# Seven products for eight in one chunk of each feed-forward product, with column blocks in pairs over eight PSUM banks, in a decoder block on Trainium2

## The chip, the cores and the metric

The kernel runs on one core of a Trainium2 chip. The metric is the device time of one execution in microseconds (us), the median of several runs. Engines are called by the names of the profile: PE (TensorE matmuls), PEld (its weight loads), DVE (VectorE), ACT (ScalarE), POOL (GpSimd), SP (SyncE, which issues most DMAs).

## The reference

One decoder block on 256 tokens of width 2048, in float32. It has two mixers side by side, a sigmoid-gated merge, an output projection, a residual and a SwiGLU feed-forward of hidden width 5632, then a final norm. The change sits in the feed-forward:

```
x1 = x + hybrid_mixer(rmsnorm(x, attn_norm_w), ...)           # 256 x 2048
h  = rmsnorm(x1, ffn_norm_w)
x2 = x1 + (silu(h @ w_gate) * (h @ w_up)) @ w_down            # 2048 -> 5632 -> 2048
out = rmsnorm(x2, final_norm_w)
```

## The kernel before

All large products run as one stream on PE. An operand `a` of a float32 product is kept as a high part (rounded to `fp32r`) and a low part (the rest), and `three` (L131) adds three products, high by high, high by low and low by high, into one PSUM bank. `Product` describes 512 output columns: for both token tiles (128 tokens each) it sums over row blocks of 128 rows of the weight, so one row block is 2 x 3 matmuls of 128 x 128 by 128 x 512. `ORDER` lists the products of the mixers; four products `wo0` to `wo3` follow, and then the feed-forward in three parts of 4, 4 and 3 hidden blocks of 512. In each part, for every hidden block `f_`, the gate product `fg` and the up product `fu` run one after the other over 16 row blocks. Four down products `fd` then run over the row blocks of that part only, and are added to the residual tiles `x1`.

`Feed` supplies the weights: `load` (L229 to L240) brings four row blocks of 512 columns (1 MB) by one DMA from SP into `wr`, of which there are three buffers. `split` (L242 to L262) takes two row blocks at a time: ACT casts them to the high part `wh` (L254) and DVE subtracts to get the low part `wl` (L255); of each there are five buffers. `split_to` keeps the splits four ahead of the products (`AHEAD`).

All else is cut into steps by generators. `Side.tick` is called after each row block, so after every six matmuls, and lets each waiting task take a step; `yield n` skips n ticks. What the traced program lists is the order on every engine: each engine runs its instructions exactly in that order, and semaphores do the rest.

A result with tokens on partitions (`g`, `x1`, `y`, the heads) has to be transposed before it can be the next product's operand. `across_task` (L158) does it in one of two ways. `transpose_task` sends eight 128 x 128 transposes through PE. `turn_task` (L182), for the kinds in `TURN`, uses `turn` (L171): 16 DVE transposes of 32 partitions x 256 elements that put each 32 x 32 block where it belongs, and then a cast on ACT and a subtraction on DVE (L189, L190; with a column scale L195, L196). `Split.ready` says when an operand is there, and `Side.until` holds back the issue of matmuls until it is.

PSUM is split into three pools: four banks for accumulators (`accp`), two for transposes (`trp`), two for attention (`atp`). `fg_done` and `fu_done` (L882 to L896) read the accumulators straight from PSUM: ACT applies silu into `g`, and DVE multiplies by the up product (L894). `fd_done` adds into `x1` (L912).

## Time and profile before

| what | value |
|---|---|
| median of 3 runs | 1752.54 us |
| lowest and highest run | 1752.49 and 1752.93 us |
| span of the profiled execution | 1750.4 us (its own time is not listed apart; the three runs lie 2.1 to 2.5 us above this span) |
| PE busy | 1739.8 us, 99% of the span, 7873 matmuls |
| DVE busy | 1217.4 us, 70% |
| ACT busy | 856.6 us, 49% |
| POOL busy | 6.3 us |
| DMA | 332.08 MB, mean 190 GB/s |
| granted PE clock | 0.9 or more of full speed in all 40 slices |

The span is the time from the first to the last instruction. Busy shares are averages over the stages. PE's matmuls are pipelined: one is listed with a length of 389 ns, but the next starts earlier, so the rate is read from starts and not from lengths.

### The profile page before, as it was taken

What the parts mean: (1) busy time and instruction counts of PE and PEld (TensorE: products, weight loads), DVE (VectorE), ACT (ScalarE), POOL (GpSimd) and SP (SyncE); (2) the same over time, 40 slices, a digit from 0 to 9 for tenths busy, and PEclk for the clock granted to TensorE, in tenths of its full rate; (3) what the DMA queues carried; (4) which work ended last, traced back from release to release, by engine and by line L of the source; (5) the groups of instructions that cost most, each with busy time, mean ns of one, the idle gap of its engine ahead of it and who ended that gap; (6) DMA issues with size and microseconds to landing.
All of it is one profiled execution on the core that took longest, in us unless ns stands there. A gap on an engine that the chain in (4) does not pass through costs nothing.

```text
span 1750.4 us, 20353 instructions
## 1 busy us (share of the span) xinstructions
PE 1739.8 (99%) x7873; PEld 1443.0 (82%) x7873; DVE 1217.4 (70%) x1838; ACT 856.6 (49%) x1103; POOL 6.3 (0%) x31
## 2 busy tenths in 40 slices
PE   9999999999999999999999999999999999999998
PEld 7888888888888888888888888888888888888886
DVE  6876877875567978876597886666546666546655
ACT  7555565644345555565444554444344444344443
POOL 1000000000000000000000000000000000000000
PEclk9999999999999999999999999999999999999999
DMA  8656555655666556555666566665566665566553
GB/s 265 215 174 192 163 174 172 180 192 195 193 194 179 175 167 187 169 172 181 212 217 204 192 206 203 193 192 193 193 194 192 194 196 195 194 193 195 196 185 106
DMA packets 169872, 332.08 MB, mean 190 GB/s; under 512 B 7584, under 2 KB 9264, under 8 KB 169776
## 3 DMA queue, kind: packets, MB, share of 16 engines
q1 hardware_dynamic: 169744, 330.78, 59.8%
q8 instruction: 61, 1.00, 0.2%
q14 instruction: 35, 0.29, 0.0%
q10 hardware_dynamic: 32, 0.01, 0.0%
HBM read 328.67 MB, written 2.10 MB: 189 GB/s over the span
## 4 chain that ended last, share of the span: by engine, by line
PE 99%; DMA 0%; DVE 0%; SPq 0%; ACT 0%; issue 0%; DVEq 0%
PE acc_fd L135 5%; PE acc_fg L134 5%; PE acc_fg L133 5%; PE acc_fu L134 5%; PE acc_fu L133 5%; PE acc_fd L133 5%; PE acc_fu L135 5%; PE acc_fg L135 5%; PE acc_fd L134 5%; PE acc_mv L133 2%; PE acc_mo L133 2%; PE acc_dq L133 2%; PE acc_gm L133 2%; PE acc_gd L133 2%; PE acc_dq L135 2%; PE acc_dk L135 2%
## 5 line engine op out<-in xcount | busy, mean ns | idle before, releaser
L255 DVE TENSOR_TENSOR wl_fg<-wr_fg,wh_fg 128x1024 fp32r<-128x1024 f32 x88 | 107.8, 1225 | 85.3 <-ACT wh_fg L254 84.7
L255 DVE TENSOR_TENSOR wl_fu<-wr_fu,wh_fu 128x1024 fp32r<-128x1024 f32 x88 | 107.6, 1225 | 80.8 <-ACT wh_fu L254 80.3
L254 ACT CAST wh_fg<-wr_fg 128x1024 fp32r<-128x1024 f32 x88 | 93.0, 1057 | 142.1 <-PE acc_fu L135 66.5
L255 DVE TENSOR_TENSOR wl_fd<-wr_fd,wh_fd 128x1024 fp32r<-128x1024 f32 x82 | 100.1, 1225 | 89.7 <-ACT wh_fd L254 89.6
L254 ACT CAST wh_fd<-wr_fd 128x1024 fp32r<-128x1024 f32 x82 | 86.2, 1056 | 122.1 <-PE acc_fd L135 96.1
L254 ACT CAST wh_fu<-wr_fu 128x1024 fp32r<-128x1024 f32 x88 | 92.6, 1054 | 96.4 <-PE acc_fg L135 48.5
L133 PE MATMUL acc_fg<-wh_fg,x1Th 128*128 128x512 f32 x352 | 136.9, 389 | 0.0
L134 PE MATMUL acc_fg<-wl_fg,x1Th 128*128 128x512 f32 x352 | 136.9, 389 | 0.0
L135 PE MATMUL acc_fg<-wh_fg,x1Tl 128*128 128x512 f32 x352 | 136.9, 389 | 0.0
L133 PE MATMUL acc_fu<-wh_fu,x1Th 128*128 128x512 f32 x352 | 136.9, 389 | 0.0
L134 PE MATMUL acc_fu<-wl_fu,x1Th 128*128 128x512 f32 x352 | 136.9, 389 | 0.0
L135 PE MATMUL acc_fu<-wh_fu,x1Tl 128*128 128x512 f32 x352 | 136.9, 389 | 0.0
L133 PEld LDWEIGHTS acc_fg<-wh_fg,x1Th 128*128 128x128 f32 x352 | 66.1, 188 | 13.7
L135 PEld LDWEIGHTS acc_fg<-wh_fg,x1Tl 128*128 128x128 f32 x352 | 66.1, 188 | 13.7
L133 PEld LDWEIGHTS acc_fu<-wh_fu,x1Th 128*128 128x128 f32 x352 | 66.1, 188 | 13.7
L135 PEld LDWEIGHTS acc_fu<-wh_fu,x1Tl 128*128 128x128 f32 x352 | 66.1, 188 | 13.7
L134 PEld LDWEIGHTS acc_fu<-wl_fu,x1Th 128*128 128x128 f32 x352 | 66.1, 188 | 13.7
L134 PEld LDWEIGHTS acc_fg<-wl_fg,x1Th 128*128 128x128 f32 x352 | 66.1, 188 | 13.6
L178 DVE STREAM_TRANSPOSE turned<-g 32x256 f32<-32x256 f32 x160 | 69.7, 435 | 2.5
L255 DVE TENSOR_TENSOR wl_bm<-wr_bm,wh_bm 128x1024 fp32r<-128x1024 f32 x32 | 39.2, 1225 | 37.4 <-ACT wh_bm L254 37.3
L178 DVE STREAM_TRANSPOSE turned<-tok_dqk 32x256 f32<-32x256 f32 x128 | 55.7, 435 | 2.1
L254 ACT CAST wh_bm<-wr_bm 128x1024 fp32r<-128x1024 f32 x32 | 33.8, 1056 | 46.6 <-PE acc_bm L135 42.4
(378 smaller groups left out, 4611.4 us busy)
## 6 DMA issues: line engine op xcount, KB each, us to landing
wr_fg<-in_w_ffn_gate_dram SPq DMA_DIRECT2D x44, 1024.0 KB, 5.2
wr_fu<-in_w_ffn_up_dram SPq DMA_DIRECT2D x44, 1024.0 KB, 5.2
wr_fd<-in_w_ffn_down_dram SPq DMA_DIRECT2D x44, 1024.0 KB, 5.1
wr_mo<-in_w_in_dram SPq DMA_DIRECT2D x16, 1024.0 KB, 5.5
wr_mv<-in_w_in_dram SPq DMA_DIRECT2D x16, 1024.0 KB, 5.4
wr_gm<-in_w_in_dram SPq DMA_DIRECT2D x16, 1024.0 KB, 5.4
wr_bm<-in_w_branch_m_dram SPq DMA_DIRECT2D x16, 1024.0 KB, 5.1
wr_dq<-in_w_in_dram SPq DMA_DIRECT2D x16, 1024.0 KB, 5.4
```

The source lines that it names most:

```text
L133: nc.tensor.matmul(o, lhsT=a[0], rhs=b[0], start=first, stop=False)
L134: nc.tensor.matmul(o, lhsT=a[0], rhs=b[1], start=False, stop=False)
L135: nc.tensor.matmul(o, lhsT=a[1], rhs=b[0], start=False, stop=last)
L178: nc.vector.transpose(out=o, in_=i)
L254: nc.scalar.copy(out=hi[:, i:i + step], in_=r)
L255: nc.vector.tensor_tensor(out=lo[:, i:i + step], in0=r, in1=hi[:, i:i + step].bitcast(F32), op=ALU.subtract)
```

## The change

Four things are done to the feed-forward, and one to all transposed results.

1. Products in pairs. `Pair` takes two column blocks at a time: gate and up of the same hidden block (11 pairs `fgu0` to `fgu10`), and two down blocks (`fd00`, `fd02`, `fd10`, `fd12`, `fd20`). The last two down blocks of the last part stay single products.
2. Seven for eight. In one chunk of four row blocks (the first), the operand's 2 x 2 quarters (two token tiles by two halves of the chunk) times the weight's 2 x 2 quarters (two halves by two column blocks) are computed as seven products of quarters or of sums of quarters (`SEVEN`), each in its own bank, P1 to P7; the other chunks add their plain products into P1 and P7 (first column block) and P2 and P8 (second). The order interleaves one of the seven with one plain operation until the seven are used up. Sums of weights are made in place in `wr` by DVE (`sum_up`, four per pair), sums of the operand by `add_up` (four additions, one cast, one subtraction, for chunk 0 of `x1T` and of each part's `gT`).
3. Evictions. `quarters` copies P3 on ACT, makes four combinations of P3 to P6 on DVE and four more DVE operations with P1, P7, P2 and P8, before silu and the multiplication (or the addition into `x1`).
4. Banks and buffers. At `fgu0` the three PSUM pools are closed and one pool of eight banks (`bankp`) is opened. `wr` has four buffers in place of three, the pool `c4` 23 in place of 25. The last hidden block's result, which went through PE transposes (`glast3`), is now of a kind in `TURN`. The final norm's weights are loaded before `fd20` and not before the first gate product.
5. `turn_task`. In place of 16 transposes of 32 partitions there are two of 128 partitions x 512 elements, which leave each 32 x 32 block on its old partitions. POOL then writes the tile to a DRAM buffer with one DMA and reads it back with four, which puts the blocks on their new partitions. The task waits four ticks between writing and reading and four between reading and use. This is done for 30 results; the two convolution inputs keep the 16 transposes.

```diff
-N_C4 = 25
+N_C4 = 23
+N_RAW = 4
+TURN_OUT, TURN_BACK = 4, 4
...
+    def feed_forward_banks():
+        banks.close()
+        late.append(ctx.enter_context(tc.tile_pool(name="bankp", bufs=8, space=PS)))
...
+        def add_up(self, g, block):
+            z = c4([P, 4, 2, P], "sums")
...
+            a11, a12, a21, a22 = (block(t, h) for t in range(2) for h in range(2))
+            for o, x, y, op in ((out[0], a12, a22, ALU.add), (out[1], a21, a22, ALU.subtract),
+                                (out[2], out[0], a21, ALU.subtract), (out[3], a11, out[2], ALU.subtract)):
+                nc.vector.tensor_tensor(out=o, in0=x, in1=y, op=op)
...
+            nc.scalar.copy(out=self.shi[g], in_=z)
+            nc.vector.tensor_tensor(out=self.slo[g], in0=z, in1=self.shi[g].bitcast(F32), op=ALU.subtract)
...
     def turn_task(src, dst, g, scale_col=None, rate=2):
-        yield 1
-        t = c4([P, 4, S], "turned")
-        yield from turn(src, t, rate)
+        yield 1
+        y = c4([P, 4, 4, TT, 32], "turned")
+        for tt in range(TT):
+            nc.vector.transpose(out=y[:, :, :, tt].rearrange("p b k s -> p k b s"),
+                                in_=src[:, tt].rearrange("p (k b f) -> p k b f", k=4, f=32))
+            yield
+        d = drp.tile([4, 32, 4, 256], F32, tag="d", name="across")
+        nc.gpsimd.dma_start(out=d.rearrange("a f b n -> (a f) (b n)"), in_=y.rearrange("p b k t s -> p (b k t s)"))
+        del y
+        yield TURN_OUT
+        t = c4([P, 4, 4 * TT, 32], "across")
+        for b in range(4):
+            nc.gpsimd.dma_start(out=t[32 * b:32 * b + 32].rearrange("p a u s -> p a (u s)"),
+                                in_=d[:, :, b].rearrange("a f n -> f a n"))
+        yield TURN_BACK
         hi, lo = dst.alloc(g)
...
+    SEVEN = (("P3", (0, 1), None, (0, 1)), ("P1", (0, 0), None, (0, 0)), ("P2", (1, 0), None, "d"),
+             ("P4", (1, 0), (1, 1), "a"), ("P5", (1, 1), (0, 1), "b"), ("P6", (0, 1), (1, 0), "c"),
+             ("P7", (0, 0), (0, 1), (1, 0)))
...
+        def sum_up(self):
+            if self.add and not self.added:
+                o, x = (feed.raw[g][:, 2 * h:2 * h + 2] for g, h in ((self.raw, self.half), self.add))
+                nc.vector.tensor_tensor(out=o, in0=o, in1=x, op=ALU.add)
+            self.added = True
+
+        def split(self):
+            self.sum_up()
...
+            nc.scalar.copy(out=hi, in_=r)
+            nxt = feed.units[feed.nsplit + 1:feed.nsplit + 2]
+            if nxt and isinstance(nxt[0], Op):
+                nxt[0].sum_up()
+            nc.vector.tensor_tensor(out=lo, in0=r, in1=hi.bitcast(F32), op=ALU.subtract)
...
+        def run(self):
+            side.push("post", self.post(self))
+            u0 = feed.units.index(self.ops[0])
+            for n, op in enumerate(self.ops):
+                feed.split_to(u0 + n + self.ahead)
+                g = op.chunk - self.g0
+                side.until(lambda: self.xt.ready[g], self.name)
+                hi, lo = op.parts
+                for j in range(2):
+                    for b, x in op.uses:
...
+                        three(self.banks[b], self.xt.quarter(g, x, j), (hi[:, j], lo[:, j]), first, self.left[b] == 0)
...
+                    if len(op.uses) == 2 or j == 1:
+                        side.tick()
...
+    def quarters(pair):
...
+        nc.scalar.copy(out=s3, in_=ps["P3"])
+        yield from pair.after("P6", 2)
+        op(u, s3, ps["P6"], ALU.subtract)
+        op(v, u, ps["P4"], ALU.add)
+        yield
+        op(x, v, ps["P5"], ALU.subtract)
+        op(u, ps["P5"], u, ALU.subtract)
+        for t, c, b, o, op_ in ((0, 0, "P1", s3, ALU.add), (1, 0, "P7", v, ALU.subtract),
+                                (0, 1, "P2", u, ALU.add), (1, 1, "P8", x, ALU.add)):
+            yield from pair.after(b, 2)
+            op(o, ps[b], o, op_)
+            yield t, c, o
```

The order of the instructions is moved everywhere in the feed-forward. Three places follow; the line numbers are each kernel's own, and the words in brackets are the engines (or DMA queues, DMASW for POOL's) that a row waits for.

First, PE where the feed-forward begins. `acc_wo3_1` is the accumulator of the last product ahead of it, `x1T` the operand. Before:

```order
L135 MATMUL acc_wo3_1_8341<-wh_wo3_8403,yTl3_7879 128x512
L133 MATMUL acc_fg0_0_8515<-wh_fg0_8427,x1Th0_8117 128x512 [waits Activation_49]
L134 MATMUL acc_fg0_0_8515<-wl_fg0_8428,x1Th0_8117 128x512 [waits DVE_49]
L135 MATMUL acc_fg0_0_8515<-wh_fg0_8427,x1Tl0_8118 128x512
L133 MATMUL acc_fg0_1_8516<-wh_fg0_8427,x1Th0_8117 128x512
```

Of the change:

```order
L181 MATMUL acc_wo3_1_8228<-wh_wo3_8294,yTl3_7807 128x512
L179 MATMUL acc_fgu0_P3_8400<-wh_fgu0_8317,x1Th0_8045 128x512 [waits DVE_49,Activation_49]
L180 MATMUL acc_fgu0_P3_8400<-wl_fgu0_8318,x1Th0_8045 128x512
L181 MATMUL acc_fgu0_P3_8400<-wh_fgu0_8317,x1Tl0_8046 128x512
L179 MATMUL acc_fgu0_P3_8400<-wh_fgu0_8317,x1Th0_8045 128x512
L180 MATMUL acc_fgu0_P3_8400<-wl_fgu0_8318,x1Th0_8045 128x512
```

The first matmul of the feed-forward now waits for DVE as well, and the one behind it, which needs DVE's `wl`, no longer has to.

Second, DVE from the end of one gate and up pair into the next (`wl` are low parts of weights, L305 sums of weights in place, `q1` and `q3` combinations, `g` the hidden block). Before:

```order
L894 SCALAR_TENSOR_TENSOR g_9013<-acc_fu1_0_9016,rs_x1_8655,g_9013 128x512 [waits PE_49]
L894 SCALAR_TENSOR_TENSOR g_9013<-acc_fu1_1_9017,rs_x1_8655,g_9013 128x512 [waits PE_49]
L255 TENSOR_TENSOR wl_fg2_9159<-wr_fg2_9072,wh_fg2_9158 128x1024 [waits DMAHW0_49,Activation_49]
L255 TENSOR_TENSOR wl_fg2_9175<-wr_fg2_9072,wh_fg2_9174 128x1024 [waits Activation_49]
L178 STREAM_TRANSPOSE turned_9186<-g_9013 32x2x4x32 [waits DVE_49]
L178 STREAM_TRANSPOSE turned_9186<-g_9013 32x2x4x32 x3
L255 TENSOR_TENSOR wl_fg2_9198<-wr_fg2_9106,wh_fg2_9197 128x1024 [waits DMAHW1_49,Activation_49]
L178 STREAM_TRANSPOSE turned_9186<-g_9013 32x2x4x32 x4
```

Of the change:

```order
L392 TENSOR_TENSOR q1_8429<-acc_fgu0_P2_8478,q1_8429 128x512
L1101 SCALAR_TENSOR_TENSOR g_8407<-q1_8429,rs_x1_8546,g_8407 128x512 [waits DVE_49]
L392 TENSOR_TENSOR q3_8431<-acc_fgu0_P8_8497,q3_8431 128x512 [waits PE_49]
L1101 SCALAR_TENSOR_TENSOR g_8407<-q3_8431,rs_x1_8546,g_8407 128x512 [waits DVE_49]
L305 TENSOR_TENSOR wr_fgu1_8677<-wr_fgu1_8677 128x1024
L317 TENSOR_TENSOR wl_fgu1_8777<-wr_fgu1_8747,wh_fgu1_8776 128x1024 [waits DMAHW7_49,Activation_49]
L317 TENSOR_TENSOR wl_fgu1_8802<-wr_fgu1_8677,wh_fgu1_8801 128x1024 [waits Activation_49]
L237 STREAM_TRANSPOSE turned_8811<-g_8407 128x4x4x32
L305 TENSOR_TENSOR wr_fgu1_8677<-wr_fgu1_8677,wr_fgu1_8605 128x1024
L317 TENSOR_TENSOR wl_fgu1_8814<-wr_fgu1_8747,wh_fgu1_8813 128x1024 [waits Activation_49]
L237 STREAM_TRANSPOSE turned_8811<-g_8407 128x4x4x32
L317 TENSOR_TENSOR wl_fgu1_8836<-wr_fgu1_8677,wh_fgu1_8835 128x1024 [waits Activation_49]
```

The evictions have doubled, sums of weights stand between the splits, and two transposes stand where there were sixteen.

Third, ACT in the first down product of the last part, where the last hidden block's operand `gT2h2` is made (`wh` are high parts of weights). Before:

```order
L254 CAST wh_fd20_13014<-wr_fd20_12928 128x1024 [waits DMAHW0_49,DVE_49,PE_49]
L254 CAST wh_fd20_13030<-wr_fd20_12928 128x1024 [waits DVE_49,PE_49]
L146 CAST gT2h2_13048<-ps_tr_13050 128x512 [waits PE_49]
L254 CAST wh_fd21_13057<-wr_fd21_12962 128x1024 [waits DMAHW1_49,DVE_49]
L254 CAST wh_fd21_13073<-wr_fd21_12962 128x1024 [waits DVE_49,PE_49]
```

Of the change, where `wh_fd20_13344` is the weight that PE multiplies with the first use of `gT2h2`:

```order
L313 CAST wh_fd20_13344<-wr_fd20_13316 128x1024 [waits DMAHW2_49,PE_49,Activation_49]
L313 CAST wh_fd20_13362<-wr_fd20_13105 128x1024 [waits DVE_49,PE_49,Activation_49]
L313 CAST wh_fd20_13375<-wr_fd20_13316 128x1024 [waits PE_49,Activation_49]
L313 CAST wh_fd20_13399<-wr_fd20_13105 128x1024 [waits DVE_49,PE_49,Activation_49]
L313 CAST wh_fd20_13412<-wr_fd20_13366 128x1024 [waits DMAHW3_49,PE_49,Activation_49]
L260 CAST gT2h2_13416<-across_13388 128x512 [waits DMASW4_49,DMASW5_49,DMASW3_49,DMASW2_49]
L260 CAST gT2h2_13416<-across_13388 128x512
```

The operand's cast waits for POOL's four DMAs instead of PE's transposes, and stands four weight casts behind the weights of its first use.

## Rows read from the trace of the kernel before

**Rows 1.** The page: busy time of each engine, and the chain that ended last by engine.
```profile
PE 1739.8 (99%) x7873; PEld 1443.0 (82%) x7873; DVE 1217.4 (70%) x1838; ACT 856.6 (49%) x1103; POOL 6.3 (0%) x31
...
PE 99%; DMA 0%; DVE 0%; SPq 0%; ACT 0%; issue 0%; DVEq 0%
```
**Rows 2.** The waits of PE: who waited <- for whom: us, times, longest.
```profile
PE ps_warm L393 <- DVE ssx L387: 1.1, 1, 1.1
```
**Rows 3.** Stages: the feed-forward: length, busy us (instructions) per engine, clock, DMA share, GB/s.
```profile
1022.40:1742.00 719.60, 719.26 (x3177) 595.39 (x3176) 445.88 (x542) 309.81 (x330) 0.00 (x0) 1.00 0.59 190
```
**Rows 4.** Timeline of PE in a down product: start us, length us, what; twelve matmuls apart.
```profile
1239.83 0.39 PE L135 MATMUL acc_fd<-wh_fd,gT0l 128*128 128x512 f32 x1
...
1242.55 0.39 PE L135 MATMUL acc_fd<-wh_fd,gT0l 128*128 128x512 f32 x1
```
**Rows 5.** Groups by form, DVE then ACT, 1064 to 1742 us: busy us, mean ns | idle before.
```profile
L255 DVE TENSOR_TENSOR wl_fu<-wr_fu,wh_fu 128x1024 fp32r<-128x1024 f32 x80 | 98.0, 1225 | 76.9 <-ACT wh_fu L254 76.4
L178 DVE STREAM_TRANSPOSE turned<-g 32x256 f32<-32x256 f32 x160 | 69.7, 435 | 2.5
L894 DVE SCALAR_TENSOR_TENSOR g<-acc_fu,rs_x,g 128x512 f32<-128x512 f32 x22 | 15.4, 744 | 0.0
L190 DVE TENSOR_TENSOR gT1l<-turned,gT1h 128x512 fp32r<-128x512 f32 x8 | 5.2, 686 | 0.0
...
L254 ACT CAST wh_fu<-wr_fu 128x1024 fp32r<-128x1024 f32 x80 | 84.3, 1054 | 92.2 <-PE acc_fg L135 48.0 <-PE acc_fu L135 44.2
L886 ACT ACTIVATE g<-acc_fg,rs_x 128x512 f32<-128x512 f32 x20 | 13.7, 690 | 9.4 <-PE acc_fg L135 9.4
L189 ACT CAST gT0h<-turned 128x512 fp32r<-128x512 f32 x8 | 4.6, 623 | 8.2 <-DVE turned L178 8.2
```
**Rows 6.** Timeline of DVE at the end of a gate and up product.
```profile
1064.54 1.23 DVE L255 TENSOR_TENSOR wl_fg<-wr_fg,wh_fg 128x1024 fp32r<-128x1024 f32 x1 [1.50 <-ACT wh_fg L254]
1065.68 1.40 DVE L894 SCALAR_TENSOR_TENSOR g<-acc_fu,rs_x,g 128x512 f32<-128x512 f32 x2
...
1069.98 1.23 DVE L255 TENSOR_TENSOR wl_fg<-wr_fg,wh_fg 128x1024 fp32r<-128x1024 f32 x1 [1.49 <-ACT wh_fg L254]
1071.12 1.78 DVE L178 STREAM_TRANSPOSE turned<-g 32x256 f32<-32x256 f32 x4
```
**Rows 7.** Timelines of ACT and of DVE: one split in a down product.
```profile
1240.25 1.06 ACT L254 CAST wh_fd<-wr_fd 128x1024 fp32r<-128x1024 f32 x1 [1.66 <-PE acc_fd L135]
...
1241.34 1.23 DVE L255 TENSOR_TENSOR wl_fd<-wr_fd,wh_fd 128x1024 fp32r<-128x1024 f32 x1 [0.30 <-ACT wh_fd L254]
```
**Rows 8.** Timeline of PE: four transposes between matmuls, in the last part.
```profile
1680.46 0.39 PE L135 MATMUL acc_fd<-wh_fd,gT2l 128*128 128x512 f32 x1
1680.70 0.60 PE L143 MATMUL ps_tr<-ident,g 128*128 128x128 f32 x4
...
1681.37 0.40 PE L134 MATMUL acc_fd<-wl_fd,gT2h 128*128 128x512 f32 x1
```
**Rows 9.** Timeline of DVE: the evictions of the last product ahead of the feed-forward.
```profile
1022.22 1.28 DVE L864 TENSOR_TENSOR x<-acc_wo,x 128x512 f32<-128x512 f32 x2
```
**Rows 10.** DMA issues: count, KB each, median us from issue to landing.
```profile
wr_fd<-in_w_ffn_down_dram SPq DMA_DIRECT2D x44, 1024.0 KB, 5.1
...
out_dram<-x SPq DMA_DIRECT2D x8, 256.0 KB, 3.1
...
fw<-in_final_norm_w_dram SPq DMA_DIRECT2D x2, 512.0 KB, 6.3
wg_raw<-in_w_in_dram SPq DMA_DIRECT2D x1, 128.0 KB, 6.2
```
**Rows 11.** DMA queue of SP (packets, MB, share of 16 engines), and what SP waited for longest.
```profile
q1 hardware_dynamic: 169744, 330.78, 59.8%
...
SPq L237 <- DVE wl_fg L255: 212.0, 42, 5.6
```
**Rows 12.** Timeline of DVE in the tail: an operation with one tensor input.
```profile
1744.15 0.88 DVE L958 TENSOR_SCALAR x<-x,f 128x512 f32<-128x512 f32 x2
```

More of the change, by code (lines that the diff above doesn't have):

```diff
@@ L1 @@
 import math
+from contextlib import ExitStack
 import concourse.bass as bass
@@ L139, in transpose_half @@
         hi, lo = dst.hi[g], dst.lo[g]
-        ps = trp.tile([P, 2, S], F32, tag="tr", name="ps_tr")
+        if late:
+            ps = late[0].tile([P, 2, S], F32, tag="bank", name="ps_tr")
+        else:
+            ps = trp.tile([P, 2, S], F32, tag="tr", name="ps_tr")
         for j in range(2):
@@ L198, in turn_task @@
+                nc.scalar.copy(out=hi[:, k:k + 2], in_=z[:, k:k + 2])
+                nc.vector.tensor_tensor(out=lo[:, k:k + 2], in0=z[:, k:k + 2], in1=hi[:, k:k + 2].bitcast(F32),
+                                        op=ALU.subtract)
             if k == 0:
                 yield
+        if g in dst.sums:
+            yield
+            if z is None:
+                dst.add_up(g, lambda tt, h: t[:, :, 4 * h:4 * h + 4].rearrange("p a (j t) s -> p t j a s", t=TT)[:, tt])
+            else:
+                dst.add_up(g, lambda tt, h: z[:, 2 * h:2 * h + 2, tt * P:(tt + 1) * P])
@@ L211, in __init__ @@
             self.hooks, self.ahead, self.by_token, self.steps = {}, AHEAD, False, {}
+    SEVEN = (("P3", (0, 1), None, (0, 1)), ("P1", (0, 0), None, (0, 0)), ("P2", (1, 0), None, "d"),
+             ("P4", (1, 0), (1, 1), "a"), ("P5", (1, 1), (0, 1), "b"), ("P6", (0, 1), (1, 0), "c"),
+             ("P7", (0, 0), (0, 1), (1, 0)))
+    class Op:
+        def __init__(self, pair, chunk, raw, half, add, uses, frees):
+            self.pair, self.chunk, self.raw, self.half, self.add = pair, chunk, raw, half, add
+            self.uses, self.frees, self.added, self.parts = uses, frees, False, None
+        def sum_up(self):
[5 more added lines that the diff above has]
+            self.sum_up()
+            r = feed.raw[self.raw][:, 2 * self.half:2 * self.half + 2]
+            hi = wp.tile([P, 2, 512], F32R, tag="wh", name=f"wh_{self.pair.name}")
+            lo = wp.tile([P, 2, 512], F32R, tag="wl", name=f"wl_{self.pair.name}")
+            nc.scalar.copy(out=hi, in_=r)
[3 more added lines that the diff above has]
+            nc.vector.tensor_tensor(out=lo, in0=r, in1=hi.bitcast(F32), op=ALU.subtract)
+            self.parts = hi, lo
+            for g in self.frees:
+                del feed.raw[g]
+                feed.load()
@@ new lines, in quarters, with op @@
+    def quarters(pair):
+        def op(o, i0, i1, op_):
+            nc.vector.tensor_tensor(out=o, in0=i0, in1=i1, op=op_)
+        ps = pair.banks
+        yield from pair.after("P3", 2)
+        s3, u, v, x = (t2([P, 512], f"q{i}") for i in range(4))
+        nc.scalar.copy(out=s3, in_=ps["P3"])
+        yield from pair.after("P6", 2)
+        op(u, s3, ps["P6"], ALU.subtract)
+        op(v, u, ps["P4"], ALU.add)
+        yield
+        op(x, v, ps["P5"], ALU.subtract)
[5 more added lines that the diff above has]
+            yield t, c, o
@@ L271, in run @@
     def run(p):
-        acc = [accp.tile([P, 512], F32, tag="acc", name=f"acc_{p.name}_{tt}") for tt in range(TT)]
+        if isinstance(p, Pair):
+            p.run()
+            return
+        acc = [bank(f"acc_{p.name}_{tt}") for tt in range(TT)]
         if p.by_token:
@@ L915, in fd_done, with down_post, task @@
         return f
+    def down_post(c, last):
+        def task(pair):
+            for got in quarters(pair):
+                if got is None:
+                    yield
+                    continue
+                t, j, q = got
+                nc.vector.tensor_tensor(out=x1[c + j][:, t], in0=x1[c + j][:, t], in1=q, op=ALU.add)
+            if last:
+                for j in range(2):
+                    side.push("fin", final_squares(c + j))
+        return task
     def weigh(c, tt):
@@ L1028, in hybrid_block @@
             side.push("param", lambda_task())
-        if p.name == "fg0":
+        if p.name == "fgu0":
+            feed_forward_banks()
+        if p.name == "fd20":
             load_fw()
```

169 lines of the change are left out of this document (124 added, 45 removed).

## The prediction

> **What bounds the kernel now.** I read the page first. PE is busy for 99% of the span, and in the chain that ended last 99% is PE and no other engine has 1% [rows 1]. Next come PE's waits: the longest is 1.1 us, at the start of the kernel, so nobody keeps PE waiting later [rows 2]. The table by stage shows that this holds in the feed-forward, where the change sits: in its 719.6 us PE is busy for 719.3, at a granted clock of 1.00, while DVE is busy for 445.9 (62%), ACT for 309.8 and the DMA engines for 59% [rows 3]. PE therefore has neither a wait nor a slow clock to give back; the feed-forward gets shorter only by fewer matmuls. Last, the groups of DVE and ACT: the idle time in front of DVE's splits ends with ACT's casts, that in front of ACT's casts with PE [rows 5], and one split shows it: ACT waits 1.66 us for PE, and DVE then 0.30 us for ACT [rows 7]. These engines follow PE and have slack. That slack must carry what the change adds.
>
> **Removed from PE.** In a down product, twelve matmuls start 1239.83 to 1242.55, so one takes 0.2267 us [rows 4]. A pair has 192 matmuls now; its first chunk of four row blocks has 48, of which seven products for eight leave 42. Sixteen pairs save 96 matmuls: 96 x 0.2267 = 21.8 us, 1.36 us per pair. A gate and up pair falls from 43.5 to 42.2 us. The eight PE transposes of the last hidden block go as well. Four of them stand between two matmuls that start 0.91 us apart in place of the 0.45 of two matmuls [rows 8]; twice 0.46 is 0.9 us.
>
> **Added at the entry.** The new pool takes over the banks of the products ahead, so PE's first matmul waits for DVE's evictions of `wo3`, which run 1.28 us from 1022.22, to 1023.5 [rows 9]. The feed-forward began at 1022.40 [rows 3]. That is +1.1 us; 0.6 if the first bank to be written is one that the first eviction freed, 2 if semaphores and a cold pipeline add to it.
>
> **Added on DVE, hidden.** Durations overlap, so I take starts: a split is followed by the next operation 1.14 us later, twice [rows 6]. Two 512-element additions from PSUM take 1.28 us [rows 9], and one lasts about 0.69 [rows 5], so they start 0.60 apart; a multiplication into `g` starts 1.40 - 0.74 = 0.66 after the one ahead [rows 5, 6]. A gate and up pair has 16 splits, 3 or 4 weight sums and three splits of summed weights, 23 operations of 1024 elements: 26.2 us. Eight combinations at 0.65 (between those two) are 5.2, two multiplications 1.3, two low parts of operands 1.2. No 128 x 512 transpose is in the trace. The four of 32 x 256 have a pitch of (1.78 - 0.435) / 3 = 0.448 us [rows 5, 6]; with twice the elements, between 0.6 (a plain 512-element operation) and eight times 0.448, that is 3.6 us. I take 0.72, near the plain operation, as such a transpose also moves one element per partition after another. The sum is 35.3 us of DVE in PE's 42.2, so I cost it at nothing; the cover is 7 us per pair, and beyond it each microsecond would cost one.
>
> The tightest place is the start of a pair. There the chain on DVE is: a cast on ACT before it (1.06 and a gap of 0.03), six operations of 1024 elements (6.8), four evictions and multiplications (2.6), two transposes (1.4): 12.0 us after the last pair's end; three more of 1024 make it 15.4, when the fifth plain split is ready. PE wants it after five of the seven products (1.36 each) and four plain operations (2.72 each): 17.7 us. The margin is 2.3 us. ACT has about 23 us of work per pair, from 19 casts at 1.06, `g` and operands [rows 5], and stays under PE. The sums of an operand (four additions, a cast and a low part) add 0.6 to 0.7 us each to DVE once per part; they come behind the fifth split, where its lead grows again, so nothing is added. The fourth buffer of `wr`, the two fewer of `c4` and the earlier load of the final weights move only work that no row shows anybody waiting for; they are costed at nothing too.
>
> **Added on POOL and the DMA queues.** Thirty results go out to DRAM (512 KB) and back, 30 MB more, so the DMA share rises from 59% to about 65%. SP waits longest for a buffer's last split on DVE (212 us over 42 times), not for bandwidth [rows 11], so the loads are not late. No DMA by POOL is in the trace. Of those by SP, 256 KB land 3.1 us after issue, 1024 KB after 5.1 [rows 10]: the way out takes 4.1. For the way back, four DMAs in short rows, I take 5.1, so the round trip is 9.2 us. Its ends: 6.2 (twice 3.1) and 12.6 (twice the 6.3 of `fw` [rows 10]); if the four came one after another, 6.3 + 4 x 6.2 = 31. It is hidden wherever the program puts the use far enough behind: writing, reading and use are eleven ticks apart, each at least six matmuls, so 15.0 us.
>
> One place has no such room: `fd20` in the last part. Its third chunk needs the hidden block that has just ended, 17.7 us after that end. The second transpose is done at 12.0, the data has landed at 21.2, the cast (0.62) and the low part (0.69) [rows 5] end at 22.5, against 18.1 (17.7 and the last matmul's own 0.39): **+4.4 us**. Even a fast trip leaves 2.6, because the operand's cast stands behind a weight cast whose buffer PE frees only at 17.7: 0.2 + 1.06 + 0.62 + 0.69. The wait is then 2.6 + (trip - 7.4); a trip of 12.6 gives 7.8. While PE waits there, ACT's and DVE's splits behind run on.
>
> On this the Trainium skill has a price: "DMA: Bandwidth & Descriptors", section "Anatomy of one DMA — SWDGE (gpsimd) path", gives a DMA by GpSimd a fixed part of some 2.0 us and the rest by bytes at 436 GB/s. As an estimate from that page each leg would take some 3 us, the wait at `fd20` would be the least one, 2.6, and the time 1733.5. No run here shows it, as POOL issues none of these before; the sum above keeps 9.2.
>
> **The sum.** -21.8 - 0.9 + 1.1 + 4.4 = -17.2 us. The profiled span of 1750.4 becomes 1733.2; runs lie 2.1 us above it, so the median of 1752.5 becomes **1735.3 us**, rounded up to 1735.5.
>
> **The rivals.**
> *A. DVE becomes the bound (slower).* Place: the two transposes in front of the next pair's splits. At 3.6 us each they add 5.8 us to the chain of 15.4, past its margin of 2.3: PE waits 3.5 us at the fifth plain split of each pair that follows a gate and up pair, 11 x 3.5 = 38 us, so 1773. It begins at 1.9 us a transpose and cancels the gain (17.2 / 11 = 1.56 us a pair) at 2.65. For it: the margin is thin, and operations that go strided through PSUM or SBUF are unseen. Against it: the transposes of 32 partitions already run near a plain operation's rate. 8%.
>
> *B. The round trip is late everywhere (slower).* ACT works in order, so an operand's cast that waits for POOL's DMAs holds back the weight casts behind it. ACT would reach it some 21.5 us after a pair's end; up to a trip of 9.5 nothing waits, up to about 15.8 the splits' lead takes it up, and beyond that each microsecond costs one in each of 11 pairs, and one at `fd20`. The gain is gone at a trip of 16.7; at 18 it is 2.2 x 11 = 24 and 8.8 at `fd20`, so 1768. For it: four DMAs in short rows, the far end of 31. Against it: all kinds of DMA rows lie between 3.1 and 6.3 us [rows 10]. 8%.
>
> The Trainium skill speaks for B in "SBUF — State Buffer", section "SBUF: two separate sides": while DVE runs an operation in its two-port mode, GpSimd cannot write the descriptors of its DMAs. This trace shows such a faster form only in the tail, where two one-input operations of 512 elements take 0.88 us [rows 12] against 0.69 for a single two-input one; between the feed-forward's transposes DVE runs two-input ones, so the rule changes little here. If it held for DVE's every operation, POOL's descriptors would come only in DVE's gaps, and the time would be that of B.
>
> *C. Part is eaten in small waits.* With seven or eight banks in use, a pair's next product finds its bank only after the combinations, and PE waits some 0.7 us (one DVE operation) at sixteen starts: +11, so 1742 to 1749. For it: the order of evictions is now longer. Against it: PE's first matmul of a later pair waits for ACT alone by the listing. 11%.
>
> *D. The saving is not there.* If the six matmuls of a quarter cost more than 0.2267 us, the 3081 that are left in the feed-forward (3177 [rows 3] less 96) take 7.1 us more for each 1.0% (0.0023 each), and 2.4% takes the whole gain: 1752. Nothing in the trace hints at it; the shapes are the same. 3%.
>
> **How the numbers follow.** My forecast has 70%. A change of 0.2% is 3.5 us, about what a measurement of this kernel can tell; so no change is 1749.0 to 1756.0. The forecast and C count as faster, and a mild A or B too: 0.70 + 0.11 + 0.02. D and half-way cases of A and B lie within 0.2%: 0.06. The rest of A and B is slower: 0.11. The range takes the short trip and the cheap entry below (1735.3 - 1.8 - 0.5, and a little less at the chunk starts: 1732.0) and the long trip (+3.4) and C above, to 1748.
>
> **What would show it.** PE has 7873 - 104 = 7769 matmuls, transposes among them, and still 0.2267 us between starts. Its waits hold one of about 1 us at the first matmul of `fgu0`, ended by DVE, and one of about 4 at `fd20`'s third chunk, ended by an operand; nothing else over 1 us. The transposes' mean is under 1.9 us; POOL's DMAs land within 4 to 5 us; DVE's busy share in the feed-forward is near 80%. I am wrong if PE waits in every pair for a low part of a weight (A) or for a high part with ACT held by POOL's DMAs (B), or if the pitch is longer (D).

## The result, and the profile after

| what | before | after |
|---|---|---|
| median of 3 runs | 1752.5 us | 1809.5 us |
| lowest to highest | 1752.5 to 1752.9 us | 1809.1 to 1814.7 us |
| profiled execution: its span | 1750.4 us | 1813.0 us |

The change makes the kernel slower: the ratio is 1.0335, with a 95% interval from 1.0316 to 1.0354. The forecast was 1735.5 us, in a range of 1732 to 1748. The profiled execution is the longest of the three, so what its trace shows adds up to some 5 us more than the medians differ by.

The page gives the busy time of each engine, and then the chain that ended last by engine:

```profile
PE 1746.1 (96%) x7769; PEld 1432.9 (79%) x7769; DVE 1262.7 (70%) x1678; ACT 911.8 (50%) x1187; POOL 88.8 (5%) x181
...
PE 75%; DVE 8%; DMA 7%; issue 7%; ACT 2%; POOL 1%; ACTq 0%; DVEq 0%; POOLq 0%
```

PE has 7769 matmuls, the number forecast, but it was 99% of the chain before [rows 1] and is 75% now. The same shows in the stage table of the feed-forward, from its start to the last matmul's start (columns as in [rows 3]):

```profile
1022.40:1803.69 781.29, 724.77 (x3073) 585.26 (x3072) 594.02 (x644) 362.02 (x405) 35.07 (x64) 0.97 0.59 192
```

The stage has grown from 719 to 781 us, with a granted clock of 0.97 where it was 1.00 [rows 3]. DVE's 594 us are 76% of it. What PE waits for (columns as in [rows 2]):

```profile
PE acc_fgu_P L180 <- DVE wl_fgu L317: 18.6, 16, 2.1
PE acc_fgu_P L179 <- ACT wh_fgu L313: 17.8, 11, 2.6
PE acc_fd_P L179 <- ACT gT2h L260: 14.5, 1, 14.5
PE acc_fd_P L180 <- DVE wl_fd L317: 2.8, 3, 1.3
PE acc_fd_P L179 <- ACT wh_fd L313: 1.8, 2, 1.4
...
PE acc_fgu_P L179 <- DVE x L1073: 1.0, 1, 1.0
```

Before, the longest wait was the 1.1 us at the start [rows 2]. Now PE waits 27 times for a low part of a weight or a high part in gate and up pairs, and once 14.5 us for the operand of the last hidden block. Behind ACT's casts stands this (the waits of ACT):

```profile
ACT wh_fgu L313 <- DVE wr_fgu L305: 96.7, 43, 4.5
...
ACT gT0h L260 <- DMA across<-across: 38.1, 4, 10.1
ACT gT1h L260 <- DMA across<-across: 36.9, 4, 9.5
ACT gT2h L260 <- DMA across<-across: 29.5, 3, 11.1
```

All 11 hidden blocks make ACT wait some 9 to 11 us for POOL's DMAs (the other, longer sum, for the weight sums on DVE, turns out below not to hold PE by itself). The first case, in the timelines of DVE, POOL, ACT and PE (start us, length us):

```profile
1082.27 0.70 DVE L237 STREAM_TRANSPOSE turned<-g 128x512 f32<-128x512 f32 x1
...
1083.27 0.56 POOL L242 DMA_DIRECT2D across<-turned  x1 [33.15 <-DVE turned L237]
1090.22 2.19 POOL L247 DMA_DIRECT2D across<-across  x4 [6.39 <-DMA across<-turned]
...
1102.04 0.62 ACT L260 CAST gT0h<-across 128x512 fp32r<-128x512 f32 x1 [9.73 <-DMA across<-across]
1102.57 1.04 ACT L313 CAST wh_fgu<-wr_fgu 128x1024 fp32r<-128x1024 f32 x1
...
1103.66 0.50 PE L179 MATMUL acc_fgu_P<-wh_fgu,x1Th 128*128 128x512 f32 x1 [1.62 <-ACT wh_fgu L313]
```

The second transpose ends at 1082.97. The way out takes until 1089.7, the four DMAs back are issued by 1091.9, and ACT gets the data at 1102.04: a round trip of 19.1 us, where 9.2 were taken. For the 11 blocks it is 17.9 to 19.2, each time up to ACT's first cast, which starts within 0.2 us of the landing. ACT then casts the weight that PE already waits for. This is rival B, at the trip that it gave as an example.

A list of the distances between PE's starts shows the whole loss. Against 0.2267 us each they are 84.9 us too long in all. 65.7 of this are single waits of over 0.25 us with the start behind them; 12.8 are 64 distances of some 0.43 us, the rate of a 1.2 GHz clock, always right after waits; here after one of 2.6 and one of 2.2 us:

```profile
1112.97 0.80 PE L180 MATMUL acc_fgu_P<-wl_fgu,x1Th 128*128 128x512 f32 x1 [2.15 <-DVE wl_fgu L317]
1113.56 0.63 PE L181 MATMUL acc_fgu_P<-wh_fgu,x1Tl 128*128 128x512 f32 x1
1113.99 0.63 PE L179 MATMUL acc_fgu_P<-wh_fgu,x1Th 128*128 128x512 f32 x1
1114.42 0.63 PE L180 MATMUL acc_fgu_P<-wl_fgu,x1Th 128*128 128x512 f32 x1
```

The granted clock of this stretch (last column but two; columns as in [rows 3]) is half of full speed:

```profile
1113.56:1117.82 4.26, 4.26 (x11) 3.34 (x10) 3.90 (x4) 0.51 (x1) 0.00 (x0) 0.50 0.86 286
```

The other 6.4 lie in distances that are only a little too long. The matmuls and transposes saved (-22.7) and these 84.9 make +62.2 of the 62.6 by which the span grew. By place: 17.0 at the last hidden block's first use, 5.2 in the first pair, about 10 in each of the three pairs that follow the first hidden block of a part, 3.1 to 4.7 in each of the seven other pairs behind a gate and up pair.

### The profile page after: what moved, and what is told of

The parts are those of the page before. It is cut to its first block, busy times and chain, and to the rows that moved or that the text cites. A ratio compares the mean times of both kernels' runs of the same rounds, so it can differ in the third digit from the quotient of the medians.

```text
span 1813.0 us, 20500 instructions
## 1 busy us (share of the span) xinstructions
PE 1746.1 (96%) x7769; PEld 1432.9 (79%) x7769; DVE 1262.7 (70%) x1678; ACT 911.8 (50%) x1187; POOL 88.8 (5%) x181
## 4 chain that ended last, share of the span: by engine, by line
PE 75%; DVE 8%; DMA 7%; issue 7%; ACT 2%; POOL 1%; ACTq 0%; DVEq 0%; POOLq 0%
DMA across<-across 5%; PE acc_fgu_P L180 3%; PE acc_fgu_P L181 3%; PE acc_fgu_P L179 3%; DVE wl_fgu L317 3%; PE acc_fd_P L180 3%; PE acc_fd_P L179 3%; PE acc_fd_P L181 3%; DMA across<-turned 2%; PE acc_mv L179 2%; PE acc_mo L179 2%; PE acc_dq L179 2%; PE acc_gm L179 2%; PE acc_dk L179 2%; PE acc_gd L179 2%
## 5 line engine op out<-in xcount | busy, mean ns | idle before, releaser
L313 ACT CAST wh_fgu<-wr_fgu 128x1024 fp32r<-128x1024 f32 x209 | 212.0, 1048 | 170.7 <-DVE wr_fgu L305 96.7
L317 DVE TENSOR_TENSOR wl_fgu<-wr_fgu,wh_fgu 128x1024 fp32r<-128x1024 f32 x209 | 250.7, 1219 | 52.9 <-ACT wh_fgu L313 49.9
L180 PE MATMUL acc_fgu_P<-wl_fgu,x1Th 128*128 128x512 f32 x594 | 237.9, 401 | 18.6 <-DVE wl_fgu L317 18.6
L179 PE MATMUL acc_fgu_P<-wh_fgu,x1Th 128*128 128x512 f32 x594 | 236.9, 399 | 18.8 <-ACT wh_fgu L313 17.8
L181 PE MATMUL acc_fgu_P<-wh_fgu,x1Tl 128*128 128x512 f32 x594 | 235.5, 396 | 0.0
L180 PEld LDWEIGHTS acc_fgu_P<-wl_fgu,x1Th 128*128 128x128 f32 x594 | 114.2, 192 | 49.0 <-DVE wl_fgu L317 25.5
L179 PEld LDWEIGHTS acc_fgu_P<-wh_fgu,x1Th 128*128 128x128 f32 x594 | 114.1, 192 | 47.8 <-ACT wh_fgu L313 22.5
L181 PEld LDWEIGHTS acc_fgu_P<-wh_fgu,x1Tl 128*128 128x128 f32 x594 | 114.3, 192 | 23.5
L247 POOL DMA_DIRECT2D across<-across x120 | 65.4, 552 | 170.2 <-DMA across<-turned 71.1
L461 DVE TENSOR_TENSOR wl_dq<-wr_dq,wh_dq 128x1024 fp32r<-128x1024 f32 x32 | 39.2, 1224 | 26.5 <-ACT wh_dq L460 26.0
```

Source lines behind the costliest of these rows:

```text
L179: nc.tensor.matmul(o, lhsT=a[0], rhs=b[0], start=first, stop=False)
L180: nc.tensor.matmul(o, lhsT=a[0], rhs=b[1], start=False, stop=False)
L181: nc.tensor.matmul(o, lhsT=a[1], rhs=b[0], start=False, stop=last)
L247: nc.gpsimd.dma_start(out=t[32 * b:32 * b + 32].rearrange("p a u s -> p a (u s)"), in_=d[:, :, b].rearrange("a f n -> f a n"))
L313: nc.scalar.copy(out=hi, in_=r)
L317: nc.vector.tensor_tensor(out=lo, in0=r, in1=hi.bitcast(F32), op=ALU.subtract)
```

## The experiments

**Is it the trip, and what without it?** Theory 1 was that the trip holds ACT in front of the weight casts. Its rivals were the weight sums on DVE, which stand in front of ACT's casts (theory 2), and late weight loads (theory 3).

*e1: the operand's casts later.*

```diff
-        yield TURN_BACK
+        yield 12 if dst.name[0] == "g" else TURN_BACK
```

> The changed kernel, with one number altered: for the hidden blocks the steps between the read back from DRAM and its use are 12 ticks in place of 4. Every instruction is the same; ACT's cast of the operand (and DVE's low part) stand eight ticks later, at least 10.9 us. Theory 1 (the trip through DRAM takes 18 to 19 us and ACT, in order, waits for it in front of the weight casts): PE's waits at the starts of the pairs go, which with the slow clock behind them are some 63 us of the 85 that the change lost against its sum; those of the first pair (5) and of the first use of the last hidden block (17) stay. Time 1745 to 1752. Theory 2 (the weight sums on DVE in front of ACT's casts, a back and forth that the sum did not price, hold each pair's start): the casts of operands don't matter, 1795 to 1815. Theory 3 (the weights land late because of the added traffic): no change, 1805 to 1815.

Measured: 1771.4 us, ratio 1.0110 (1.0095 to 1.0125), 38 us less than the change. PE's waits now:

```profile
PE acc_fd_P L179 <- ACT gT2h L260: 14.3, 1, 14.3
PE acc_fgu_P L180 <- DVE wl_fgu L317: 5.0, 5, 2.0
PE acc_fd_P L179 <- ACT gT0h L260: 2.8, 1, 2.8
PE acc_fd_P L179 <- ACT gT1h L260: 1.7, 1, 1.7
```

PE's waits for ACT's weight casts are gone with nothing moved but the operand's casts and what follows them (its low part and its sums), so the weight sums on DVE alone don't hold the pairs: theories 2 and 3 fall as the main cause. The trip is as long as before, and what waits now is each part's last hidden block, whose use is near. The miss of some 20 us is, by the places of the waits, these, the bursts of operand sums, and a longer matmul (below).

*e2: no trip at all.* `turn_task` is that of the kernel before (16 transposes of 32 x 256), with the sums of chunk 0 behind it.

> The changed kernel with its part 5 undone: all results are turned by 16 DVE transposes of 32 partitions, nothing goes through DRAM; pairs, seven products and eight banks stay. Theory 1: all waits for the trip go, the one at the last hidden block too. DVE gets 5.8 us more per gate and up pair (41 of 42.2 us), so either nothing is late (1731 to 1738) or PE waits up to 3.5 us in each of 11 pairs (1770). Theory 2 (DVE's chain at the pair's start is what is late): 5.8 us longer in each pair, above 1815. Theory 3: 1730 to 1745.

Measured: 1804.3 us, ratio 1.0297 (1.0282 to 1.0313). PE's longest sums:

```profile
PE acc_fgu_P L180 <- DVE wl_fgu L298: 28.6, 29, 2.2
PE acc_fd_P L179 <- ACT gT2h L238: 8.5, 1, 8.5
```

In an ordinary pair PE's starts are 0.6 + 1.8 + 0.9 us late, 3.3 in all, against the 3.5 that the working of rival A gave for 5.8 us more on DVE. The DVE arithmetic holds, then; the time comes to more than 1770 since the last hidden block (8.5 us, a wait that theory 1 had expected to go), the operand sums and the slow clock add to it. The change needs its cheaper transposes, and their price is the trip.

*e3: the trip in the kernel before.* The new `turn_task` and a DRAM pool, nothing else of the change.

> The kernel before with part 5 alone: the results go through DRAM as in the change; no pairs, three weight buffers, old banks, the last hidden block by PE. If the trip is slow in itself (18 us), it exceeds the 15 us of eleven ticks, ACT is held some 3 us for each hidden block, part of it covered by the splits' lead: 1755 to 1790. If it is slow only because two or three weight loads of 1 MB are issued together in the changed kernel, it takes 12 to 16 us here and nobody waits: 1750 to 1756. Theory 2: 1752.5, whatever the trip takes.

Measured: 1780.3 us, ratio 1.0157 (1.0140 to 1.0174). Neither case came out pure. Nine of the ten hidden blocks' trips take 11.8 to 12.4 us and most make nobody wait. But three uses are close behind their result: the last chunk of `x1T` (PE waits 9.7 us; trip 1034.3 to 1047.6, 13.3 us), the last block of the first part (8.0) and of the second (2.5). The last block of the first part has the one long trip, 17.3 us; 2.4 of these are a pause of POOL between its second and third read, for which the profile names no cause. So the trip's length depends on the kernel around it, and at a near use even 12 to 13 us are too long.

*e4: e1, and the very last block by 16 DVE transposes.*

```diff
-            side.push("tr", across_task("g", g, gT, i))
+            side.push("tr", turn16_task(g, gT, i, None, 4) if gT.name == "gT2" and i == 2 else across_task("g", g, gT, i))
```

> As the first of these runs, and the last hidden block alone is turned by 16 DVE transposes. Theory 1: against the first run the 14.5 us wait at its first use and the slow clock after it (17 us in all) shrink to 2 to 6 us: 1731 to 1740. Theory 2: as the first run, 1785 to 1805. Theory 3: 1790 to 1810.

Measured: 1764.9 us, ratio 1.0065 (1.0043 to 1.0087), runs from 1755.9 to 1767.5. The profiled one is the lowest; in it the wait for `gT2h` is 1.1 us in place of 14.3. The direction is as expected, but the median is still 25 us or more over the expected 1731 to 1740, and what the longer runs lost is not seen in the lowest one's trace.

**Where does the seven-for-eight chunk come in?**

*e5:* e4 with the last block of every part and all of `x1` by 16 transposes, and the four sums one per tick.

> As the last run, and three more places are taken off the trip: the last hidden block of every part and the four blocks of x1 are turned by 16 DVE transposes, so the trip stays for eight hidden blocks (and the results of the mixers) whose use is far off; the four sums of an operand are made one per tick and not in one burst. Theory 1: what is left of PE's waits is the entry (1.1) and some 2 to 8 us where DVE's extra transposes or sums meet the splits: 1731 to 1742, faster than the kernel before. Theory 2 (the back and forth of weight sums and casts holds the pairs): 1755 to 1770 as the last run. If 16 transposes at a pair's start are more than DVE can hide even in three pairs: 1745 to 1755.

*e6:* e5 without seven for eight. *e7:* the changed kernel without it:

```diff
-list(range(4)), {0}, f"fgu{f_}",
+list(range(4)), set(), f"fgu{f_}",
...
-list(range(f0, f1)), {f0},
+list(range(f0, f1)), set(),
```

and `quarters` hands P1, P7, P2 and P8 on as they are.

> The run above without seven for eight: the first chunk is eight plain products, no sums of weights or operands, no combinations; pairs, eight banks and the same way of turning stay. Theory 1: 96 matmuls more at 0.2267 us, less the waits that sums and combinations cause there: 1750 to 1757, some 12 to 22 us above the run above. If the sums cost more than the matmuls that they save: below the run above.

> The changed kernel without seven for eight, the trip as the change has it. Theory 1 (trip): the trip still exceeds the ticks, so PE still waits in the pairs that follow a gate and up pair; the waits are shorter, since four splits ahead are 10.9 us of plain operations against 8.2 of mixed ones and no burst of sums stands behind the casts: 22 us more matmuls, 25 to 45 us fewer waits, 1785 to 1810, and the wait at the last hidden block stays over 8 us. Theory 2 (the sums hold the pair's start): the waits at the pairs' starts go, 1765 to 1780.

Measured: e5 1762.2 us (1.0064, 1.0050 to 1.0077), e6 1756.5 us (1.0023, 1.0014 to 1.0032), e7 1757.4 us (1.0032, 1.0020 to 1.0044). e5 missed its 1731 to 1742: PE waits 11.9 us for weights' low parts in the down pairs, where the 16 transposes now stand. e6, without the seven, comes out below e5, so there the sums cost more than the matmuls that they save. e7 refuted what theory 1 had said of it: with the trip's steps as the change has them, PE's only waits in the feed-forward are the entry (1.0 us) and 0.4 for `gT2h`. The data of its 11 blocks land 9.5 to 13.4 us after the second transpose. Nor does theory 2 explain that, after e1. So the seven products lengthen the trip. What differs is the weight loads. In e7 SP issues one about every 5.4 us. In the change the seven hold two of the four buffers to their end, and then three buffers come free within 4 us: five loads start between 1082 and 1094 (1082.4, 1085.3, 1089.9, 1091.5 and 1093.8), while the trip runs from 1083 to 1102. The DMA issues of that stretch (count, KB, median us from issue to landing), with what all queues moved:

```profile
DMA packets 2707, 5.78 MB, mean 275 GB/s; under 512 B 143, under 2 KB 143, under 8 KB 2706
...
wr_fgu<-in_w_ffn_gate_dram SPq DMA_DIRECT2D x3, 1024.0 KB, 12.7
...
across<-turned POOLq DMA_DIRECT2D x1, 512.0 KB, 6.4
across<-across POOLq DMA_DIRECT2D x4, 128.0 KB, 9.7
```

*e8: a trip in quiet.* At the end of the kernel before, with no weight load left, one trip that nobody waits for.

> The kernel before, with one trip of 512 KB more and nothing else: late in the last product, when no weight load is left, ACT copies a tile, POOL writes it to DRAM by one DMA and reads it back by four; nobody waits for it. If the 18 us of the trip are its own price, the way out takes 6 to 7 us here too and each DMA of the way back 8; if it is the company of weight loads, the way out takes about 3 us and the way back 2 to 4. The time stays within 5 us of the kernel before.

Measured: 1752.4 us in one run. The trip's DMAs:

```profile
across<-turned POOLq DMA_DIRECT2D x1, 512.0 KB, 3.1
across<-across POOLq DMA_DIRECT2D x4, 128.0 KB, 4.9
```

Alone, the way out takes half as long as in the change; the way back ran beside the output's stores and took more than the 2 to 4 us expected.

**Is it the company of the loads?** (theory 4)

*e9: the same instructions in another order.* The four plain operations of the second chunk first, and the seven behind them.

```diff
-            order = []
+            order, plain = (plain[:4], plain[4:]) if self.name != "fd20" else ([], plain)
```

> The changed kernel with another order inside a pair and nothing else: the four plain operations of the second chunk come first, and only then one of the seven alternates with one plain operation (in the last part's first pair the order stays). All instructions, sums, buffers and steps of the trip are the same, but the three weight loads that the seven release together, at their end, are now issued some 11 us later in the pair, behind the trip. Theory 4 (the seven hold two weight buffers to their end, so three loads of 1 MB go out together just when the trip is under way, and the trip takes 18 to 19 us in place of 12): the trip takes 11 to 14 us, PE's waits at the pairs' starts go, those of the first pair and of the last hidden block (17 us, perhaps a few less) stay: 1748 to 1762. Theory 2 (the back and forth between sums on DVE and casts on ACT makes the splits late): sums and casts are as many, the waits move with them into the middle of the pair: 1790 to 1812. Theory 5 (both are needed): between, 1765 to 1785.

Measured: 1758.5 us, ratio 1.0033 (1.0020 to 1.0047): 51 us less than the change by order alone. The same trip (1084 to 1096):

```profile
DMA packets 1072, 2.53 MB, mean 211 GB/s; under 512 B 96, under 2 KB 96, under 8 KB 1071
...
across<-turned POOLq DMA_DIRECT2D x1, 512.0 KB, 3.3
across<-across POOLq DMA_DIRECT2D x4, 128.0 KB, 3.4
```

The data of this trip land 9.1 us after the second transpose, and in all ten reordered places after 9.1 to 11.3; ACT, still busy with weight casts, takes them up at 10.3 here. `fd20` kept its order, and in the same run its trip still takes 18.8 us, with four loads beside it (1680 to 1700):

```profile
wr_fd<-in_w_ffn_down_dram SPq DMA_DIRECT2D x4, 1024.0 KB, 11.5
across<-turned POOLq DMA_DIRECT2D x1, 512.0 KB, 6.4
across<-across POOLq DMA_DIRECT2D x4, 128.0 KB, 8.9
```

PE waits 15.8 us there, and nowhere else in the feed-forward over 2. Theory 4 had forecast this; the sums on DVE and the casts are as many as in the change. The new order also takes the weight sums away from the pair's start, and ACT's waits for those of the gate and up pairs fall from 96.7 us to 32.2; that these alone don't hold PE is e1's showing and not e9's.

*e10: loads in twos, without seven for eight.*

```diff
-uses, [(ch, blk)] if h else []))
+uses, [(ch, 0), (ch, 1)] if h and blk else []))
```

> The changed kernel without seven for eight (as in the run that took 1757.4), with one more alteration: the two weight buffers of a chunk are released together at the chunk's end, so loads go out in twos. Theory 4: the trip grows from 12 to 14 to 17 us, and where it passes 15 us ACT waits, PE a little: 1758 to 1775. If loads in company don't matter to the trip: it stays 12 us and the time is 1757 to 1759.

Measured: 1757.2 us (1.0027, 1.0016 to 1.0038), but SP still issues one load every 5.4 us: each load waits for its own buffer's last reader, whatever is released in the listing. It says nothing on theory 4.

*e13: e9 with the trip moved into the loads.*

```diff
-        yield 1
+        yield 14 if dst.name[0] == "g" and g < len(dst.hi) - 1 else 1
```

> As the run with the plain operations first (1758.5 us, trips of 10 us), and one number altered: for all hidden blocks but the last of a part the task waits 14 ticks in place of 1 before its two transposes, so that the trip falls into the stretch 30 to 45 us after the pair's start, where that kernel issues four or five weight loads within 10 us. Instructions are the same. Theory 4 (loads in company make the trip long, and ACT in order passes the delay on to the weight casts): in these eight blocks the trip takes 16 to 20 us again, ACT waits for it up to 8 us each, PE's waits come back in the middle of the pairs: 1765 to 1800. If the trip was shortened by anything else in the new order (its place behind the pair's start, fewer waits of ACT), it stays near 10 us and the time within 2 us of 1758.5.

Measured: 1760.7 us (1.0049, 1.0032 to 1.0066). The first block's trip (1094 to 1113):

```profile
wr_fgu<-in_w_ffn_gate_dram SPq DMA_DIRECT2D x2, 1024.0 KB, 11.2
across<-turned POOLq DMA_DIRECT2D x1, 512.0 KB, 2.9
across<-across POOLq DMA_DIRECT2D x4, 128.0 KB, 9.0
```

The way out missed the loads and is short; the way back met them and takes 9.0 us in place of 3.4, while the instructions are the same. Half of the expectation held: loads in company make the way back more than twice as long. The eight moved trips take 13.7 to 15.6 us, not 16 to 20, and ACT did not wait, because one long leg alone stays under the 16 to 17.5 us that its casts stand behind the transposes.

**When the trip's packets move.** The DMA rows of the traces say more on theory 4. In the change SP issues a load 0.89 us ahead of the way out, which starts at 1083.27:

```profile
1082.38 0.37 SPq L433 DMA_DIRECT2D wr_fgu<-in_w_ffn_up_dram  x1
```

The queues (packets, MB, share of 16 engines; q1 is SP's, q0 POOL's) from 1083.27 to 1087.18, from 1087.18 to 1089.30, and on the way back from 1093.03 to 1101.19:

```profile
q1 hardware_dynamic: 432, 0.88, 88.0%
...
q0 software_dynamic: 144, 0.52, 60.4%
...
q1 hardware_dynamic: 800, 1.60, 72.8%
q0 software_dynamic: 191, 0.52, 30.5%
```

In e9, from 1085.96 to 1087.80, 1.12 us after the issue of the way out:

```profile
q0 software_dynamic: 144, 0.52, 87.2%
```

In the change no packet of the way out moves for 3.9 us, while SP's load goes through; then they take 2.1 us, against 1.8 in e9. So the way out is not slowed to half its rate: it starts late, behind a single load. The first packet comes 3.6 to 4.1 us after the issue in all 11 trips of the change, where the load is 0.89 us ahead, 2.6 to 2.9 us in e3's ten (1.48 us ahead), and 1.1 us in e7's 11 (3.6 us ahead) and in e9's ten reordered ones (7.7 us ahead). DVE is not what holds it: it is busy throughout, in the 3.9 us of the change as in the 1.1 us of e9. On the way back the packets do mix with those of the loads, which move three times as many bytes in these 8.2 us.

**Where the longer matmul comes from, and a version that is faster.**

*e11: e7 with the buffers of the value pool 4352 bytes apart.* `vap` gives tiles of 1088 elements, of which views are used.

> The changed kernel without seven for eight, and the buffers of the value pool, where the change puts the third and fourth operand block of a hidden part, are 4352 bytes apart per partition in place of 4128. In the down products with these blocks a matmul took 0.234 us in place of 0.2267, 3.3 us in all. If that comes from where the buffers begin: 0.2267 again and 1754; if it comes from anything else that these products do: 1757.4 and 0.234 as before.

Measured: 1753.5 us, ratio 1.0006 (0.9997 to 1.0016), 3.9 us under e7. In a down product, with the third operand block, twelve matmuls apart, e7 has

```profile
1226.65 0.39 PE L179 MATMUL acc_fd_P<-wh_fd,gT0h 128*128 128x512 f32 x1
...
1229.43 0.40 PE L179 MATMUL acc_fd_P<-wh_fd,gT0h 128*128 128x512 f32 x1
```

and e11

```profile
1226.67 0.39 PE L182 MATMUL acc_fd_P<-wh_fd,gT0h 128*128 128x512 f32 x1
...
1229.39 0.39 PE L182 MATMUL acc_fd_P<-wh_fd,gT0h 128*128 128x512 f32 x1
```

2.78 against 2.72 us; over the two whole chunks of e6's `fd00` with the third and fourth block the mean was 0.234, and e11 has 0.2267 in all of `fd00` and `fd02`.

*e12: the change with e9's order, e11's buffers, and the very last block turned on PE.*

> The changed kernel with seven for eight, plain operations first as in the first of these runs, the padded value buffers, and the very last hidden block turned on PE (two groups of four transposes, 0.9 us) in place of the trip. Theory 4: of PE's waits the entry (1.1) and some 3 to 5 us in the first pair stay: 1729.8 + 1.1 + 0.9 + 4, so 1733 to 1742, faster than the kernel before. Theory 2: 1770 to 1795. Theory 5: 1745 to 1765.

Measured: 1737.7 us, ratio 0.9917 (0.9902 to 0.9931), faster than both. PE's waits, all that are over 0.3 us:

```profile
PE acc_fgu_P L182 <- ACT x1Th L268: 1.4, 1, 1.4
PE ps_warm L605 <- DVE ssx L599: 1.1, 1, 1.1
PE acc_fgu_P L184 <- DVE x1Tl L269: 1.0, 1, 1.0
PE acc_fgu_P L182 <- DVE x L1076: 1.0, 1, 1.0
```

From the last matmul ahead of the feed-forward to its own last one e12 takes 702.1 us, in place of 719.1 in the kernel before: 17.0 less, close to the 17.2 of the forecast's sum, though in another kernel than the one forecast. It is 15.9 us faster than e11, which has no seven for eight (and the last block by the trip).

## Why the prediction was wrong, point by point

- **What bounds the kernel, and the matmuls saved:** right. Outside waits, and but for operand blocks in the value pool, matmuls still start 0.2267 us apart, so the 22.7 us are saved; with the waits gone, e12 shows them.
- **The entry, +1.1 us:** right. PE's first matmul starts 1.13 us late, ended by DVE.
- **DVE and its cover:** right. The 128 x 512 transpose takes 0.70 us (0.72 taken), and e2's 3.3 us per pair meet the margin of 2.3 us. Rival A did not come, as the change has no long transposes. Nor did C: but for the entry, no pair's first matmul waits.
- **The round trip, 9.2 us: the step that failed.** "For the way back, four DMAs in short rows, I take 5.1, so the round trip is 9.2 us", with ends of 6.2 and 12.6 for the range. e9's shortest trips take 9.1, so 9.2 is about what a trip costs without loads in its way; in the change it is 18 to 19. The legs were priced from transfers that had the queues almost to themselves, one load at a time [rows 10], and the change's own effect on the loads was dismissed with "so the loads are not late". They were not late. They came in the trip's way: one goes out 0.9 us ahead of the way out, and three around the start of the way back (1089.9 to 1093.8 in the first block), since the seven give three buffers back at their end.
- **What rules the sharing.** By the rows above, the way out took 3.1 us alone, 3.3 with a load issued just behind it, and 6.4 with one issued 0.9 us ahead of it and a second one behind. The Trainium skill says in "DMA: Bandwidth & Descriptors", section "Queues, rings and completion order", that each engine goes round the queues that have work, packet by packet. The way back of the change agrees in so far as both queues' packets move side by side, POOL's with 30.5% of the engines' time; the way out does not, as none of its packets moves for 3.9 us, and no run here shows why. In the same page of the Trainium skill, section "Anatomy of one DMA — SWDGE (gpsimd) path", the fixed 2.0 us and the rate for a GpSimd DMA give some 3.2 us for the way out, as an estimate: that agrees with the quiet 3.1, and not with 6.4.
- **Rival B: the mechanism was right, its chance of 8% and its price were not.** At a trip of 18 it gave 1768. Its 2.2 us per pair, 2.1 to 3.4 by its formula at the trips of 17.9 to 19.2 that came, stand beside the 3.1 to 4.7 of ordinary pairs. Left out were the operand sums, for which ACT waits a second time right behind the trip (about 10 us in place of some 4 in three pairs), 4 us in the first pair, and in all of these the lower clock after the waits, 12.8 us together.
- **`fd20`, +4.4 us:** the formula 2.6 + (trip - 7.4) gives 14.2 at the trip of 19.0 that came there; the wait was 14.5, and 17.0 with the clock behind it. The size was wrong by the trip.
- **Operand blocks in the value pool, not priced:** 3.3 us. The diff shows them there; nothing in the trace of before shows that it matters. It is rival D in a small part: a longer matmul, but in the third and fourth block of a part and not in the quarters.

Left open: e13 shows one leg, not a whole trip, stretched by loads with nothing else changed; that both legs and ACT's wait come together is seen in the change, in e1 (both legs, with ACT's wait moved away) and in `fd20` of e9 and e13. Why the way out waits for the load ahead of it is not shown.

## What to carry to other kernels

A latency read in a trace belongs to the traffic around it: before a transfer is priced, list what the change itself makes go out at the same time or just ahead of it, and in particular which buffers it sets free together. An in-order engine that must wait for such a transfer should have its waiting instruction stand behind the longest trip and not the usual one. And the order of the same instructions was worth 51 us here, more than the arithmetic that the change saved.

## What the runs showed of the hardware

- DMAs of two queues: a 512 KB write to DRAM by POOL took 3.1 us alone and 6.4 when SP had issued a 1 MB load 0.9 us ahead of it; most of the difference is that its first packet moved 3.9 us after the issue and not 1.1 to 1.3. The four 128 KB reads took 3.4 us each in e9 and 9.7 in the change, where three loads were issued around their start.
- After waits of 2.6 and 2.2 us PE's matmuls came every 0.43 us in place of 0.2267, with a granted clock of 0.50, which is the 1.2 GHz level, for ten matmuls, and then at the old rate. After waits of 1.4 and 0.8 us the same was seen at one pair's start (1433) and not at another's (1480).
- Matmuls whose stationary operand lies in buffers 4128 bytes apart per partition took 0.232 to 0.235 us (mean of a chunk), with 4352 bytes 0.2267. The weight load itself was listed with 0.19 us in e6, in these products and in others. That it is where the buffers begin is shown by e11; which offset it is was not tried.
